# Row maxima of a 256 MB matrix: one load queue in place of two, and a last tile that ends in both of its rows

## The chip, the cores and the metric

The kernel runs on one core of a Trainium2 chip. The metric is the device time of that core in microseconds (us). Before the change three runs gave 630.47, 630.69 and 630.90, a median of 630.69. One further execution is recorded by the hardware profiler, and the profile below is that one.

## The reference

The input `x` is a float32 matrix of 8192 rows and 8192 columns, 268 MB. The output is one float32 for each row: the largest absolute value in it.

```python
def reference(x):
    return np.linalg.norm(x, ord=np.inf, axis=1)
```

Every element is read from memory once and takes part in one comparison. 32 KB are written.

## The kernel before

**Tiling.** The 8192 rows are spread over the 128 partitions of the on-chip memory (SBUF), 64 rows to a partition. A tile `t` holds two rows of each partition (`B` = 2), 16384 columns of 4 bytes, so 8.39 MB. There are 32 tiles. Three buffers of the pool `sbuf` take turns (`BUFS` = 3), and each has 16 spare columns at its end (`PAD`). A buffer is loaded again when the reduce of its last use has ended.

**Bulk.** The first 24 tiles (six groups of four, `A` = 6 and `G` = 4) are loaded by one transfer each at L146. VectorE (DVE in the profile) then reduces each with one instruction at L139, `reduce_max` with absolute values, to two results per partition in `r_bulk`. L145 chooses the queue of the load. Tiles 1 to 11 are issued by ScalarE, which has no other work, and tile 0 and tiles 12 to 23 by SyncE (SP). The 48 results per partition are stored at L151, from ScalarE.

**Tail.** The last eight tiles are loaded in pieces, on SP, at L159. The list `TAIL` gives the widths of the pieces: a tile's 16384 columns are the two rows one after the other, and `segments` cuts a piece at the border between the rows. Each segment gets a reduce of its own. For the first fifteen rows of the tail the partial maxima go to `part`, one column for each segment; a reduce of 15 x 4 values makes `r_tail` of it, and ScalarE stores it at L171. The last row's partial maxima are written into the spare columns behind the row itself, so that the final reduce, `r_fin`, takes the last load and the six partial maxima in one instruction. SP stores it at L179.

**What orders the work.** Each engine works through its instructions in the order of the program. SP does nothing but issue transfers. A load waits on SP for its buffer to come free. A transfer announces its landing on one of eight semaphores, handed out in turn, and so it also waits for the transfer that had the same semaphore eight transfers earlier. The stores count among these.

**Start and end.** `start_first_load_early` moves SP's first load ahead of the barrier at the program's start. `finish_on_pool` lets the GpSimd engine wait for the last store. Both stay as they are.

Of the kernel before, what the change touches and what calls it, by code (L numbers as in the profile page):

```python
# [1 line left out]
logging.getLogger("concourse").setLevel(logging.ERROR)  # L3

# [1 line left out]

# [4 lines left out]

F32 = mybir.dt.float32
X = mybir.AxisListType.X

TAIL = [
    [2944, 13440],
    [4096, 12288],
    [11520, 4864],  # L20
    [7680, 8704],
    [6528, 3328, 6528],
    [4864, 4096, 3328, 4096],
    [3968, 3584, 3328, 2944, 2560],
    [2432, 2176, 1920, 1664, 1536, 1280, 1152, 1024, 1152, 1024, 1024],
]


def segments(loads, cols):

    out, at = [], 0
    for i, w in enumerate(loads):
        end = at + w
        while at < end:
            r = at // cols
            to = min(end, (r + 1) * cols)
            out.append((i, r, at - r * cols, to - at))
            at = to
    return out


def start_first_load_early(nc):


    sp = mybir.EngineType.SP
    first, *rest = nc.main_func.blocks
    for block in rest:
        insts = block.instructions
        for i, ins in enumerate(insts):
            if ins.engine == sp and type(ins).__name__ == "InstDMACopy":  # L50
                assert not ins.sync_info.on_wait
                moved = insts[i]
                block.instructions = insts[:i] + insts[i + 1 :]
                head = first.instructions
                at = next(k for k, h in enumerate(head) if h.engine == sp)
                first.instructions = head[:at] + [moved] + head[at:]
                return


def finish_on_pool(nc):  # L60

    sp, pool = mybir.EngineType.SP, mybir.EngineType.Pool
    body, end = nc.main_func.blocks[-2:]
    last_store = [
        i
        for i in body.instructions
        if i.engine == sp and type(i).__name__ == "InstDMACopy"
    ][-1]  # L70
    lane = last_store.sync_info.on_update[0].id
    insts = end.instructions
    src = next(i for i in insts if i.engine == sp)
    assert type(src).__name__ == "InstDrain" and not src.sync_info.on_update
    at = next(k for k, i in enumerate(insts) if type(i).__name__ == "InstISA")
    drain, clear = insts[at - 1], insts[at]
    assert drain.engine == clear.engine == pool
    assert type(drain).__name__ == "InstDrain"
    assert not (drain.sync_info and drain.sync_info.on_wait)
    waits = sorted(src.sync_info.on_wait, key=lambda s: s.id == lane)  # L80
    assert waits[-1].id == lane
    wait = mybir.InstDrain(
        name=nc.get_next_instruction_name(),
        engine=pool,
        ins=[],
        outs=[],
        sync_info=mybir.SyncInfo(on_wait=waits, on_update=[]),
    )
    moved = {src.name, drain.name, clear.name}
    end.instructions = [i for i in insts if i.name not in moved] + [wait, clear]  # L90


@with_exitstack
def kernel(
    ctx: ExitStack,
    tc: tile.TileContext,
    x: bass.AP,
    out: bass.AP,
    G: int = 4,
    B: int = 2,  # L100
    BUFS: int = 3,
    PAD: int = 16,
):
    nc = tc.nc
    P = nc.NUM_PARTITIONS
    rows, cols = x.shape
    W = B * cols


    n_tail = B * len(TAIL)  # L110
    n_bulk_rows = rows // P - n_tail
    assert n_bulk_rows % (G * B) == 0
    A = n_bulk_rows // (G * B)
    split = n_bulk_rows * P
    x_b = x[:split].rearrange("(a p n b) c -> a n p (b c)", p=P, a=A, n=G, b=B)
    out_b = out[:split].rearrange("(a p n b) -> p a (n b)", p=P, a=A, n=G, b=B)
    x_t = x[split:].rearrange("(p t b) c -> t p (b c)", p=P, b=B)
    out_t = out[split:].rearrange("(p t) -> p t", p=P)

    sbuf = ctx.enter_context(tc.tile_pool(name="sbuf", bufs=BUFS))  # L120
    outp = ctx.enter_context(tc.tile_pool(name="outp", bufs=1))

    segs = [segments(loads, cols) for loads in TAIL]
    count = {}
    for i, s in enumerate(segs):
        for _, r, _, _ in s:
            count[i * B + r] = count.get(i * B + r, 0) + 1
    n_last = count[n_tail - 1]
    k_max = max(count[r] for r in range(n_tail - 1))
    assert n_last - 1 <= PAD  # L130

    r_bulk = outp.tile([P, A, G * B], F32)
    r_tail = outp.tile([P, n_tail], F32)
    r_fin = outp.tile([P, 1], F32)
    part = outp.tile([P, n_tail - 1, k_max], F32)
    nc.vector.memset(part[:], 0.0)  # L136

    def absmax(o, i):
        nc.vector.reduce_max(out=o, in_=i, axis=X, apply_absolute_value=True)  # L139

    for a in range(A):
        for n in range(G):
            t = sbuf.tile([P, W + PAD], F32, tag="t")
            i = a * G + n
            queue = nc.scalar if 1 <= i < A * G // 2 else nc.sync  # L145
            queue.dma_start(out=t[:, :W], in_=x_b[a, n])  # L146
            absmax(
                r_bulk[:, a, n * B : (n + 1) * B],
                t[:, :W].rearrange("p (b c) -> p b c", b=B),
            )  # L150
    nc.scalar.dma_start(out=out_b, in_=r_bulk[:])  # L151

    seen = {}
    for i, loads in enumerate(TAIL):
        t = sbuf.tile([P, W + PAD], F32, tag="t")
        todo = segs[i]
        at = 0
        for j, w in enumerate(loads):
            nc.sync.dma_start(out=t[:, at : at + w], in_=x_t[i][:, at : at + w])  # L159
            at += w  # L160
            for _, b, c, n in [s for s in todo if s[0] == j]:
                r = i * B + b
                k = seen.get(r, 0)
                seen[r] = k + 1
                lo = b * cols + c
                if r < n_tail - 1:
                    absmax(part[:, r, k : k + 1], t[:, lo : lo + n])
                    if r == n_tail - 2 and k == count[r] - 1:

                        absmax(r_tail[:, : n_tail - 1], part[:])  # L170
                        nc.scalar.dma_start(  # L171
                            out=out_t[:, : n_tail - 1], in_=r_tail[:, : n_tail - 1]
                        )
                elif k < n_last - 1:
                    absmax(t[:, W + k : W + k + 1], t[:, lo : lo + n])
                else:

                    absmax(r_fin[:], t[:, lo : W + n_last - 1])
    nc.sync.dma_start(out=out_t[:, n_tail - 1 :], in_=r_fin[:])  # L179
    nc.at_finalize(start_first_load_early)  # L180
    nc.at_finalize(finish_on_pool)


# [1 line left out]
_INS = ['x']  # L185
_OUTS = [((8192,), 'float32')]


# [23 lines left out]
```

## Time and profile before

| | before |
|---|---|
| median of three runs | 630.69 us |
| profiled execution, device time | 630.47 us |
| profiled execution, span from first to last instruction | 628.3 us |
| VectorE busy | 551.5 us, 88% of the span |
| 24 bulk reduces (L139, 128x16384) | 411.9 us, 17214 ns each |
| 31 reduces into `part` | 130.2 us |
| 6 reduces into the last tile, and `r_fin` | 7.9 us and 1.2 us |
| VectorE idle before bulk reduces, waiting for loads | 73.4 us |
| mean rate of the transfers | 427 GB/s |
| share of SP's queue and of ScalarE's | 65.3% and 34.1% of 16 engines' span |

The page gives busy time and idle time for each engine, and rows of 40 slices in which a digit is the busy share in tenths. A group of instructions is shown with the line of the code, the engine, what is written from what, the shape, and what ended the idle time before it. A transfer has a time of issue and a time from issue to landing, which includes its turn in the queue. The names SPq and ACTq stand for the instruction queues of SP and ScalarE. The profiled execution's device time is 2.2 us longer than its span.

### The profile page before, as it was taken

The numbers are of one execution on the slowest core, as the hardware profiler recorded it, in microseconds if no ns is written. First come the engines' busy times: TensorE is split into PE (matmuls) and PEld (weight loads), VectorE is DVE, ScalarE is ACT, GpSimd is POOL, SyncE is SP. The second block draws the span as 40 slices with busy tenths as digits, with TensorE's granted clock in tenths as the row PEclk, the third lists the DMA queues.
The fourth block names the chain that finished last, engine by engine and source line by source line (L and its number), as shares of the span: only waits on it lengthen the run. The fifth ranks groups of instructions, "written<-read, shape, count | busy, mean of one in ns | idle before, by whom it ended". The sixth has DMA issues, their size and how long they took to land.

```text
span 628.3 us, 202 instructions
## 1 busy us (share of the span) xinstructions
DVE 551.5 (88%) x64; POOL 0.2 (0%) x4
## 2 busy tenths in 40 slices
DVE  0059999999998880799999999988889999999998
POOL 0000000000000000000000000000000000000000
DMA  9999999999999999999999999999999999999997
GB/s 401 467 401 467 401 451 417 413 455 413 455 421 446 421 446 426 442 401 455 413 451 417 446 421 446 421 446 421 434 432 410 439 440 423 424 433 429 424 423 299
DMA packets 8993, 268.48 MB, mean 427 GB/s; under 512 B 1952, under 2 KB 1952, under 8 KB 3104
## 3 DMA queue, kind: packets, MB, share of 16 engines
q1 hardware_dynamic: 6480, 176.16, 65.3%
q10 hardware_dynamic: 2512, 92.31, 34.1%
q14 instruction: 1, 0.01, 0.0%
HBM read 268.44 MB, written 0.03 MB: 427 GB/s over the span
## 4 chain that ended last, share of the span: by engine, by line
DVE 62%; DMA 32%; another core or an unknown queue 3%; issue 2%; SPq 0%
DVE r_bulk L139 47%; DMA t<-in_x_dram 32%; DVE part L139 14%; DVE t L139 1%; DVE r_fin L139 0%; SPq L159 0%; DVE r_tail L139 0%
## 5 line engine op out<-in xcount | busy, mean ns | idle before, releaser
L139 DVE TENSOR_REDUCE r_bulk<-t 128x2 f32<-128x16384 f32 x24 | 411.9, 17214 | 73.4 <-DMA t<-in_x_dram 73.4
L139 DVE TENSOR_REDUCE part<-t 128x1 f32<-128x8192 f32 (+18 forms) x31 | 130.2, 4272 | 0.7 <-DMA t<-in_x_dram 0.6
L139 DVE TENSOR_REDUCE t<-t 128x1 f32<-128x1152 f32 (+3 forms) x6 | 7.9, 1387 | 0.0
L139 DVE TENSOR_REDUCE r_fin<-t 128x1 f32<-128x1030 f32 x1 | 1.2, 1226 | 0.0
L136 DVE MEMSET part<- 128x60 f32 x1 | 0.1, 108 | 0.9 <-PEq L196 0.9
L139 DVE TENSOR_REDUCE r_tail<-part 128x15 f32<-128x60 f32 x1 | 0.2, 216 | 0.0
L196 POOL MEMSET const-bfloat16-1.0<- 128x1 bf16 x1 | 0.1, 101 | 0.0
L196 POOL MEMSET const-uint8-127<- 128x1 uint8 x1 | 0.1, 101 | 0.0
L196 POOL MEMSET const-float32-0.0<- 128x1 f32 x1 | 0.1, 98 | 0.2 <-issue 0.2
L196 POOL MEMSET const-float32-1.0<- 128x1 f32 x1 | 0.1, 98 | 0.0
## 6 DMA issues: line engine op xcount, KB each, us to landing
t<-in_x_dram SPq DMA_DIRECT2D x1, 6720.0 KB, 40.4
t<-in_x_dram SPq DMA_DIRECT2D x2, 3264.0 KB, 26.3
t<-in_x_dram SPq DMA_DIRECT2D x3, 2048.0 KB, 28.7
t<-in_x_dram SPq DMA_DIRECT2D x1, 6144.0 KB, 40.6
t<-in_x_dram SPq DMA_DIRECT2D x1, 5760.0 KB, 35.2
t<-in_x_dram SPq DMA_DIRECT2D x3, 1664.0 KB, 32.3
t<-in_x_dram SPq DMA_DIRECT2D x2, 2432.0 KB, 32.4
t<-in_x_dram SPq DMA_DIRECT2D x1, 4352.0 KB, 43.0
```

Of the source, the lines that this page charges most:

```text
L136: nc.vector.memset(part[:], 0.0)
L139: nc.vector.reduce_max(out=o, in_=i, axis=X, apply_absolute_value=True)
L196: nc = _bacc.Bacc("TRN2", target_bir_lowering=False, num_devices=1)
```

## The change

All 24 bulk loads are issued by SP (L145 in the new file), so ScalarE issues only the store of the bulk results.

The tail's first seven tiles have new piece widths. The last tile leaves the list `TAIL` and gets the list `LAST` of 13 loads, each of one row alone: four of row 0, seven of row 1, and then one last load of 640 columns for each row. These two are placed at the end of the buffer, row 0's first, each followed in SBUF by that row's partial maxima (four and seven). The final reduces of the two rows take the last load and the partial maxima together, and write straight into `r_tail`.

The reduce of `part` to `r_tail` (14 x 4 values now) stands behind the first piece of the last tile. One store on SP takes all 16 tail results of each partition; the store of fifteen rows on ScalarE and `r_fin` go.

```diff
 TAIL = [
-    [2944, 13440],
-    [4096, 12288],
-    [11520, 4864],
-    [7680, 8704],
-    [6528, 3328, 6528],
-    [4864, 4096, 3328, 4096],
-    [3968, 3584, 3328, 2944, 2560],
-    [2432, 2176, 1920, 1664, 1536, 1280, 1152, 1024, 1152, 1024, 1024],
+    [9728, 6656],
+    [5632, 10752],
+    [9600, 6784],
+    [9344, 7040],
+    [6784, 6528, 3072],
+    [4736, 3072, 4224, 4352],
+    [3968, 2432, 3072, 2944, 1792, 2176],
 ]
+LAST = (
+    [(0, w) for w in (2176, 2048, 1664, 1664)]
+    + [(1, w) for w in (1536, 1280, 1152, 1024, 896, 896, 768)]
+    + [(0, 640), (1, 640)]
+)
...
-            i = a * G + n
-            queue = nc.scalar if 1 <= i < A * G // 2 else nc.sync
-            queue.dma_start(out=t[:, :W], in_=x_b[a, n])
+            nc.sync.dma_start(out=t[:, :W], in_=x_b[a, n])
...
+    t = sbuf.tile([P, W + PAD], F32, tag="t")
+    left = parts_of[:]
+    col = [0] * B
+    at, slot = 0, {}
+    ends = [w for _, w in LAST[-B:]]
+    lo = W - sum(ends)
+    for b in range(B):
+        slot[b] = lo + ends[b]
+        lo = slot[b] + parts_of[b]
+    for j, (b, w) in enumerate(LAST):
+        final = left[b] == 0
+        to = slot[b] - w if final else at
+        frm = b * cols + col[b]
+        nc.sync.dma_start(out=t[:, to : to + w], in_=x_t[len(TAIL)][:, frm : frm + w])
+        col[b] += w
+        if final:
+            r = n_tail - B + b
+            absmax(r_tail[:, r : r + 1], t[:, to : slot[b] + parts_of[b]])
+        else:
+            left[b] -= 1
+            k = slot[b] + left[b]
+            absmax(t[:, k : k + 1], t[:, to : to + w])
+            at += w
+        if j == 0:
+            absmax(r_tail[:, : n_tail - B], part[:])
+    nc.sync.dma_start(out=out_t, in_=r_tail[:])
-    nc.sync.dma_start(out=out_t[:, n_tail - 1 :], in_=r_fin[:])
```

## The prediction

> **What bounds the kernel now.** I read the page from the top: busy shares and slices first, then the waits of the vector engine, then the order of time around the one long wait, then the queue's own waits, then the end.
>
> ```profile
> span 628.3 us, 202 instructions
> DVE 551.5 (88%) x64; POOL 0.2 (0%) x4
> DVE  0059999999998880799999999988889999999998
> DMA  9999999999999999999999999999999999999997
> HBM read 268.44 MB, written 0.03 MB: 427 GB/s over the span
> ```
>
> The DMA row is full in every slice but the last, while the vector engine (DVE) starts two slices late and has thin places. So the input stream sets the time: what counts is when the last load lands, and what follows it. DVE idle time costs nothing unless it delays a load. In order of time, DVE alone, the steady state and the odd place:
>
> ```profile
> 196.70 17.22 DVE L139 TENSOR_REDUCE r_bulk<-t 128x2 f32<-128x16384 f32 x1 [2.13 <-DMA t<-in_x_dram]
> 215.98 17.22 DVE L139 TENSOR_REDUCE r_bulk<-t 128x2 f32<-128x16384 f32 x1 [2.06 <-DMA t<-in_x_dram]
> 254.69 85.72 DVE L139 TENSOR_REDUCE r_bulk<-t 128x2 f32<-128x16384 f32 x5 [21.49 <-DMA t<-in_x_dram]
> ...
> 449.75 17.22 DVE L139 TENSOR_REDUCE r_bulk<-t 128x2 f32<-128x16384 f32 x1 [2.08 <-DMA t<-in_x_dram]
> 469.15 17.22 DVE L139 TENSOR_REDUCE r_bulk<-t 128x2 f32<-128x16384 f32 x1 [2.18 <-DMA t<-in_x_dram]
> ```
>
> Where DVE waits for each tile, tiles come 19.3 to 19.4 us apart ((469.15-411.10)/3 = 19.35 us, the start at 411.10 being the same view's). DVE needs 17.2. All 32 tiles at 19.35 would take 619.2 us. The last load, issued at 615.19, took 9.9 and landed at 625.1; so 5.9 us were lost somewhere. At 215.98 the queues change hands: the last load of ScalarE's queue (issued 194.60, 60.1 us to landing) and the first of SP's (issued 213.94, 40.9) share the engines and land together at 254.7 and 254.8. DVE is starved for 21.49 us, so it frees the next buffer late, and SP issues its third load of this series only at 271.94, with the load before it (issued 233.23, 40.7) landing at 274.0. The windows show what that does:
>
> ```profile
> 256.00:272.00 16.00, 16.00 (x2) 0.00 (x0) 1.00 1.04 451
> 272.00:278.00 6.00, 6.00 (x1) 0.00 (x0) 1.00 0.90 350
> 278.00:294.00 16.00, 16.00 (x2) 0.00 (x0) 1.00 1.05 455
> ```
>
> The last two columns are DMA share and GB/s: for 6 us the stream runs at 0.90 and 350. (Short windows read some 20 GB/s to either side of the 433 that 8.39 MB in 19.35 us make.) By landings the hole is 271.94+22.84 = 294.78 against 273.96, that is 20.82 us for one tile: 1.45 more than 19.37. No later tile gives it back. The other losses: start, 2.5 (two loads landed by 41.2 against 38.7); the fifth and sixth tile, 0.6 (80.02 to 119.32 against 38.7); the eight tail tiles, 1.2 (469.13 to 625.14 against 154.8). With 1.45 that is 5.75 of the 5.9.
>
> SP's own waits, and the end:
>
> ```profile
> SPq L159 <- DMA t<-in_x_dram: 62.6, 19, 7.4
> SPq L159 <- DMA out_dram<-r_bulk: 25.5, 1, 25.5
> ```
>
> SP stood 25.5 us behind the bulk store (486.40, 60.5 us to landing). This is a wait for the semaphore that the store had used, eight transfers earlier in the program. One load of 6528 columns was still queued (issued 521.01, 33.5 to landing: 554.5) when the store landed at 546.9, so the stream did not dry up.
>
> ```profile
> 621.71 3.59 DVE L139 TENSOR_REDUCE t<-t 128x1 f32<-128x1024 f32 x3
> 625.34 1.23 DVE L139 TENSOR_REDUCE r_fin<-t 128x1 f32<-128x1030 f32 x1
> 626.59 0.34 SPq L179 DMA_DIRECT2D out_dram<-r_fin  x1
> ```
>
> The last reduce starts 0.20 us after the last landing (625.14), held by the reduce before it (ends 625.30); it ends at 626.57; the store issues at 626.59, lands 1.41 later at 628.00, and the span ends at 628.27.
>
> **What the Trainium skill says.** "DMA: Bandwidth & Descriptors", Issuing engines are not separate DMA queues: transfers from several engines run on the same 16 DMA engines and interleave. The trace agrees: the twelfth and thirteenth load land 0.17 us apart, and neither queue alone is slower than both (19.32 us a tile on ScalarE's, 19.35 on SP's). Same page, Queues, rings and completion order: each engine takes turns between queues. That fits the 60.5 us of a 24 KB store behind six loads. "VectorE: DVE Perf Modes", The perf-mode tier table: `tensor_reduce` has only the 1x program, so the cost follows the element count; here (8678-1208)/(8192-1024) = 1.042 ns an element and 0.141 us fixed, of which about 0.08 overlaps the neighbour (six reduces of 8.32 in sum were busy 7.91).
>
> **The change, part by part.**
>
> *All 24 bulk loads on SP.* Removed: eleven issues on ScalarE (0.33 us each, hidden). Added: eleven on SP, in order, each behind its buffer wait. SP has nothing else to do, so what queues behind them is only the next load. Tile k+3 is issued when DVE ends tile k, 17.24 us after k landed; two tiles, less 17.2 us of progress, are still queued: 38.7-17.2 = 21.5 us of work. This is the state of 409 to 469 in the trace (issue to landing 40.7), with no hole. There is no handover any more, so two loads never land together, and the hole of 1.45 goes. At the start loads land singly: the first near 22 us instead of 38.8. DVE then starts early and idles 2.1 us a tile; hidden by the stream, worth nothing. Bounds: 0 if a hole comes elsewhere, -1.45 for this one, -2.1 if the 0.6 of the fifth and sixth tile goes too (seen only while ScalarE's queue ran, cause unknown). I take **-1.45**.
>
> *New tail pieces.* The tail has 34 loads instead of 31. Eleven loads in the last tile cost 19.67 against 19.35: 0.03 a load; **+0.1**. I followed the new widths through, at 1.195 ns a column for the stream and the reduce prices above, with three buffers and the wait for the transfer eight before. The second load of the fifth tail tile (6528) now stands behind the bulk store. The store again has six loads beside it (5632 to 7040), and a load of 6784 columns (8.1 us) is in the queue when it lands; before it was 6528 (7.7 us). The cover is as good. DVE last waits for a landing at the start of the seventh tail tile and then keeps a backlog of 0.1 to 0.5 us, two small reduces of slack.
>
> *The last two loads.* Reduces of 768 and 640 columns take 0.86 and 0.73 us start to start, against landings 0.77 apart, so the last reduce starts about 0.35 after the last landing (0.20 before). It has 640+7 elements: 0.141+0.674 = 0.815 us, instead of 1.23. From last landing to end of reduce: 1.17 instead of 1.43, **-0.26**. Both final reduces also wait for DVE's own earlier writes; those are at least one reduce back, so I count nothing; if they break the overlap it is +0.16.
>
> *One store.* ScalarE's store of fifteen rows goes (it took 5.3 us beside the loads, off the path; the 0.22 us reduce before it moves ahead in the tile). The final store has 64 bytes a partition instead of 4. No row shows such a store on idle engines; between 0 and +0.2, set against up to 0.1 regained from the store that no longer cuts into the last loads. I take **0**.
>
> Sum: -1.45+0.10-0.26 = -1.61. The profiled execution took 630.47 (span 628.27 and 2.2 around it), so 628.9; the median shown is 0.22 higher, so about **629.0**. A difference under 0.2% (1.26 us) can't be told from none.
>
> **Rivals.**
>
> (a) *The hole is not regained*: a single queue gets a hole of the same size elsewhere, at a tail issue say, or the last engine lags anyway. Then only the end improves, -0.16: 630.5. For it: the trace has unexplained slow places (the 0.6). Against: none in the stretch 294 to 469, where SP works alone.
>
> (b) *The slow place goes as well*: another -0.6 to -0.7, 628.3. For: it is only in ScalarE's stretch. Against: ScalarE's stretch from 119 to 216 runs at 19.32.
>
> (c) *Slower: SP is stuck behind the bulk store until the stream is dry.* Place: the wait of the 6528-column load. If the store lands as the 6784-column load does, the next load meets empty engines. Price: an issue 2.0 us before the running load landed cost 1.45, so an issue at its landing costs about 3.5; -1.61+3.5 gives 632.6. It decides against the change from a store about 7.5 us later than the end of the 7040-column load. For: packets of the six loads differ in size, so the turns fall differently. Against: the total beside the store is the same (six loads), and it would have to lose nearly a whole further load.
>
> (d) *The change does not do what it says*: the new final reduces wait for each other and the end gains nothing; with the hole closed that is 629.2, inside the forecast.
>
> **How the numbers follow.** Forecast with (d) 0.58, (b) 0.14, (a) 0.18, (c) 0.08, other mishaps 0.02. The likeliest case has 628.4 to 629.7; (b) reaches 628.0, (a) 630.6; the range 628.0 to 630.6 leaves out (c) and little else. Faster means under 629.43: most of the forecast and all of (b), 0.68. Within 0.2%: the forecast's upper edge and (a), 0.22. Slower: (c) and mishaps, 0.10.
>
> **What would show it.** Right: every bulk tile waits 2.1 us for its load, starts 19.35 apart from the first (near 22 us) to the twenty-fourth (near 467.5); no idle of 21 us, no window at 350 GB/s in mid-stream; last landing near 623.8; last reduce about 0.82 us, its end 1.2 after that landing; span near 626.7. Wrong: a bulk start over 20 us after its neighbour, a DMA share under 0.95 before the end (near 547 for (c)), DVE waiting in the last tile, or a final store well over 1.41 us.

## The result, and the profile after

| | before | after |
|---|---|---|
| median of six runs, us | 630.94 (630.47 to 632.19) | 627.98 (627.73 to 628.23) |
| profiled execution, device time, us | 630.47 | 628.23 |
| its span, us | 628.3 | 626.4 |

The change makes the kernel faster: the ratio is 0.9949, with a 95% interval of 0.9936 to 0.9962, which is 3.0 us in the medians. The forecast was 629.0, from 628.0 to 630.6. The direction was right; the gain was under-estimated by about 1 us, and the measured time lies just under the lower end. Already visible in the table: the times before are spread over 1.7 us, those after over 0.5.

The page after, the same lines as shown of before (a row of digits is the busy share in tenths, in 40 slices):

```profile
span 626.4 us, 204 instructions
DVE 552.9 (88%) x67; POOL 0.2 (0%) x4
DVE  0588988889988889888898888988889999999998
DMA  9999999999999999999999999999999999999997
HBM read 268.44 MB, written 0.03 MB: 429 GB/s over the span
```

The transfers are still what fills the time, and DVE is as busy as before (552.9 us against 551.5). It starts one slice earlier and is idle evenly, not in lumps. The order of time of DVE shows it:

```profile
215.62 17.22 DVE L140 TENSOR_REDUCE r_bulk<-t 128x2 f32<-128x16384 f32 x1 [2.08 <-DMA t<-in_x_dram]
234.99 17.22 DVE L140 TENSOR_REDUCE r_bulk<-t 128x2 f32<-128x16384 f32 x1 [2.15 <-DMA t<-in_x_dram]
254.34 17.22 DVE L140 TENSOR_REDUCE r_bulk<-t 128x2 f32<-128x16384 f32 x1 [2.12 <-DMA t<-in_x_dram]
273.64 17.22 DVE L140 TENSOR_REDUCE r_bulk<-t 128x2 f32<-128x16384 f32 x1 [2.08 <-DMA t<-in_x_dram]
293.00 17.22 DVE L140 TENSOR_REDUCE r_bulk<-t 128x2 f32<-128x16384 f32 x1 [2.14 <-DMA t<-in_x_dram]
...
466.99 17.22 DVE L140 TENSOR_REDUCE r_bulk<-t 128x2 f32<-128x16384 f32 x1 [2.14 <-DMA t<-in_x_dram]
```

Each tile waits some 2.1 us for its load. The wait of 21.49 us is gone, and the last bulk tile starts at 466.99, where it started at 469.15 before. The three windows of which the middle one read 350 GB/s before (last two columns: DMA share, GB/s):

```profile
256.00:272.00 16.00, 15.55 (x1) 0.00 (x0) 1.00 0.95 414
272.00:278.00 6.00, 4.36 (x1) 0.00 (x0) 1.00 1.13 492
278.00:294.00 16.00, 13.86 (x2) 0.00 (x0) 1.00 0.94 406
```

These windows do not measure a hole, neither here nor in the prediction. The stream is made of packets of 64 KB, which take 2.42 us each on one of 16 engines, and a window counts a packet in full where it starts. A window of 6 us therefore holds two packets of each engine, 350 GB/s, or up to three, 524. Over all 38 us the kernel before reads 437 GB/s with its hole, and the changed one 423 without. What shows the hole is the landings: 273.96 and 294.78 before, 20.8 us apart, and 273.61 and 292.98 now, 19.4 apart (DVE starts 0.02 to 0.03 us after each of these two). Among SP's waits, the one for the bulk store is nearly as long as before:

```profile
SPq L158 <- DMA out_dram<-r_bulk: 24.3, 1, 24.3
```

The store landed at 543.3 (issued 484.24, 59.1 us), while a load that landed at 552.7 was still in the queue. The end, in order of time:

```profile
617.90 5.31 DVE L140 TENSOR_REDUCE t<-t 128x1 f32<-128x1152 f32 x5
623.13 1.55 DVE L140 TENSOR_REDUCE r_tail<-t 128x1 f32<-128x644 f32 x2
624.71 0.35 SPq L192 DMA_DIRECT2D out_dram<-r_tail  x1
```

The last load was issued at 614.70 and landed after 8.9 us, at 623.61. The two final reduces run from 623.13 to 624.68 without a gap, and the store of all 16 results lands 1.4 us after its issue.

### The profile page after: what moved, and what is told of

Same layout as the page of the kernel before. It is cut to its first block, busy times and chain, and to the rows that moved or that the text cites. A ratio compares the mean times of both kernels' runs of the same rounds, so it can differ in the third digit from the quotient of the medians.

```text
span 626.4 us, 204 instructions
## 1 busy us (share of the span) xinstructions
DVE 552.9 (88%) x67; POOL 0.2 (0%) x4
## 4 chain that ended last, share of the span: by engine, by line
DMA 63%; DVE 35%; issue 1%; another core or an unknown queue 0%; DVEq 0%
DMA t<-in_x_dram 63%; DVE r_bulk L140 24%; DVE part L140 8%; DVE t L140 3%; DVEq L220 0%; DVE r_tail L140 0%
## 5 line engine op out<-in xcount | busy, mean ns | idle before, releaser
L140 DVE TENSOR_REDUCE part<-t 128x1 f32<-128x8192 f32 (+20 forms) x28 | 121.6, 4410 | 0.9 <-DMA t<-in_x_dram 0.8
L140 DVE TENSOR_REDUCE t<-t 128x1 f32<-128x1664 f32 (+8 forms) x11 | 16.5, 1572 | 0.0
L140 DVE TENSOR_REDUCE r_tail<-t 128x1 f32<-128x644 f32 (+1 forms) x2 | 1.5, 814 | 0.0
```

## Experiments

The theory at this point (A in the expectations, L once it is narrowed to the late issue): the two queues of the kernel before cause the loss, in one place. When ScalarE's last load and SP's first overlap they land together; DVE is starved, the next buffer comes free late, and a load is issued when the stream is nearly dry. Below, the *lead* of a load is the time from its issue to the landing of the load before it, and its *hole* is what its landing comes late: its time from issue to landing, less the lead, less the 19.35 us of a tile. The rivals: the time is saved in the tail (B), or the hole belongs to the change of queue itself and not to the late issue (Q). Times of the kernel before that stand in a comparison were measured beside the run they are compared with.

### The two halves of the change

One queue, all else as before:

```diff
-            queue = nc.scalar if 1 <= i < A * G // 2 else nc.sync
+            queue = nc.sync
```

> The kernel before with one edit: all bulk loads on SP; tail and stores as before. Theory A (the two queues cost the time: a hole of 1.45 us at the handover and 0.6 in the fifth and sixth tile): span about 626.3, no DVE wait over 3 us after the first tile, tiles 19.35 apart throughout, 2.0 to 2.5 us less than the kernel before. Theory B (the time is saved in the tail and at the end, the queues do not matter): same time as before, within 0.3 us, with another hole somewhere in the stream.

Measured: 628.28 us (628.02 to 628.64) against 631.13 for the kernel before, ratio 0.9958 (0.9945 to 0.9972): 2.85 us less. The span of the profiled execution is 626.7, the longest wait after the first tile 2.3 us. B falls: the choice of queue alone has nearly the whole gain, and somewhat more than I expected. Some 0.3 us of it lies outside the span, as the last experiment takes up.

The other half, the new tail with the old queues:

```diff
-            nc.sync.dma_start(out=t[:, :W], in_=x_b[a, n])
+            i = a * G + n
+            queue = nc.scalar if 1 <= i < A * G // 2 else nc.sync
+            queue.dma_start(out=t[:, :W], in_=x_b[a, n])
```

> The changed kernel with the old choice of queues: tiles 1 to 11 on ScalarE, the new tail, the last tile with two final reduces and one store. Theory A: the 21 us wait at the thirteenth tile and the window at 350 GB/s two tiles later are back; 0.2 to 0.5 us less than the kernel before, all of it at the end. Theory B: 2 us or more less than before.

Measured: 630.22 us against 631.13, ratio 0.9990 (0.9982 to 0.9998). The hole is back, 1.8 us in this profile. The 0.9 us is more than expected; the interval allows 0.1 to 1.1. About 0.3 of it lies outside the span here too: the device time is 1.8 us longer than the span in all 13 runs of this kernel, mostly 2.0 to 2.2 in those of the kernel before.

The kernel before once more, for a second profile:

> The kernel before, unchanged, for a second profile on the chip of the other runs and for the spread of its time. Theory A: the hole two tiles after the handover is there again, 1.4 us or more, and if its time is 1 us longer than in the first profile, the hole or the slow place after the start is what grew. Theory B: the time varies in other places.

Measured: 630.87 us, ratio 0.9999 (0.9991 to 1.0007). The hole is again at the load issued at 271.9, but bigger (columns: queue, number, us to landing):

```profile
t<-in_x_dram SPq DMA_DIRECT2D x1, 23.7
```

In the first profile it took 22.8, so the hole is 2.35 instead of 1.45. The slow place in the fifth and sixth tile, 0.6 before, is under 0.1 here. So the same code has holes of different size, and the slow place is not in every execution.

### Is it the late issue?

Two handovers from a full queue:

```diff
-            queue = nc.scalar if 1 <= i < A * G // 2 else nc.sync
+            queue = nc.scalar if 4 <= i < 15 else nc.sync
```

> The kernel before with the queue of the bulk loads changed twice from a full queue: tiles 0 to 3 on SP, 4 to 14 on ScalarE, 15 to 23 on SP. Theory A (a change of queue lets two loads land together, starves DVE for 21 us, and the next buffer comes free only 2 us before the stream is dry): two waits of 21 us, two holes of about 1.4 us each, none of the slow start; 2.9 us slower than the run with one queue, about 0.6 to 0.9 slower than the kernel before. Theory B: the same time as before. If the hole was an accident of one place, one hole at most.

Measured: 629.67 us, 1.5 us less than before (ratio 0.9981, 0.9971 to 0.9991), and 1.4 more than with one queue, of which 0.3 lies outside the span. Both waits are there, 20.91 and 21.48 us. But the first handover, from SP to ScalarE, left a lead of 2.6 us and no hole; the second left 2.0 us and a hole of 0.6. My expectation was wrong: two handovers are not two holes.

Next, all as before, but the buffer freed 2.1 us earlier by leaving columns out of one reduce:

```diff
+            cut = 1024 if i == 11 else 0
             absmax(
                 r_bulk[:, a, n * B : (n + 1) * B],
-                t[:, :W].rearrange("p (b c) -> p b c", b=B),
+                t[:, :W].rearrange("p (b c) -> p b c", b=B)[:, :, : cols - cut],
             )
```

> The kernel before, queues as before; only the reduce of the twelfth tile (the last on ScalarE's queue) leaves out the last 1024 columns of both rows, 2048 of 16384, so that DVE frees its buffer 2.1 us earlier and the next load is issued about 4.1 us instead of 2.0 us before the stream would be dry. Theory L (the hole is the late issue): the two loads still land together and DVE still waits 21 us, but the hole is gone; 2.0 to 2.6 us less than the kernel before. Theory Q (the hole belongs to the change of queue itself): the hole stays, the time within 0.3 us of before.

Measured: 628.59 us against 631.11, ratio 0.9958 (0.9946 to 0.9971), 2.5 us less. In its order of time on DVE the starved wait is unchanged:

```profile
215.44 17.22 DVE L139 TENSOR_REDUCE r_bulk<-t 128x2 f32<-128x16384 f32 x1 [2.07 <-DMA t<-in_x_dram]
254.15 83.59 DVE L139 TENSOR_REDUCE r_bulk<-t 128x2 f32<-128x14336 f32 x5 [21.48 <-DMA t<-in_x_dram]
```

and the load issued when the shortened reduce ended, at 269.3, has no hole:

```profile
t<-in_x_dram SPq DMA_DIRECT2D x1, 23.5
```

Its 23.5 us are the lead of 4.2 and the 19.35 of a tile. The queues, the handover and the 21 us of idle DVE are those of before. Only the issue came 2.1 us earlier, and the hole went. So it is the late issue (L), not the change of queue, and a 21 us wait of DVE by itself costs nothing here.

The opposite, the buffer freed 2.2 us later:

```diff
+            if i == 11:
+                absmax(part[:, 0, 0:1], t[:, :2048])
```

> The kernel before, queues as before; DVE reduces 2048 columns of the twelfth tile a second time (2.2 us, into a place that is written again later), so that the next load is issued when the stream is just running dry. Theory L: the hole grows by about the same 2.2 us, to about 4.5; 2 us slower than before. Theory Q: the hole keeps its size, since DVE has idle time enough; time within 0.3 us of before.

Measured: 631.49 us against 631.11, ratio 1.0004 (0.9996 to 1.0012), the same within its interval. The lead is -0.2 us, and the load took

```profile
t<-in_x_dram SPq DMA_DIRECT2D x1, 22.0
```

from issue to landing, just as the first load of a kernel with one queue does (21.9 to 22.1); the hole is 2.8. I had expected a hole of 4.5 and 2 us more. Leads of 2.0 showed up to 2.35 in the profiles so far, and the medians differ by 0.4: the loss does not follow the lateness one for one. Taken alone, this run is nearer to what Q forecast (within 0.3); what speaks against Q is the shortened reduce above and the run with one queue below.

Two points between:

```diff
-            cut = 1024 if i == 11 else 0
+            cut = 256 if i == 11 else 0
```

> The kernel before; the reduce of the twelfth tile leaves out the last 256 columns of both rows, so that the next load is issued 2.5 us before the stream would be dry. Theory L with a limit between 2.0 and 2.6 us (an issue 2.6 us ahead lost nothing in the run with two handovers): no hole or one under 0.3 us, 2 us or more less than before. If the loss falls evenly from 2.0 to 4.2 us: a hole of 1.0 to 1.8 us is left.

Measured: 630.90 us against 631.04, ratio 0.9994 (0.9987 to 1.0002). With a lead of 2.5 the load took

```profile
t<-in_x_dram SPq DMA_DIRECT2D x1, 24.7
```

so the hole is 2.8, as big as in the run where the stream did run dry. The sharp limit between 2.0 and 2.6 that I expected is not there.

```diff
-            cut = 1024 if i == 11 else 0
+            cut = 576 if i == 11 else 0
```

> The kernel before; the reduce of the twelfth tile leaves out the last 576 columns of both rows, so that the next load is issued about 3.2 us before the stream would be dry. If the limit is at the time from issue to a new load's first packets, [...]no hole and 628.6; if the loss falls slowly up to 4.2 us, a hole of 0.5 to 2 us.

Measured: 629.19 us against 630.90, ratio 0.9969 (0.9958 to 0.9979). A lead of 3.2 and a hole of 0.4 in the profile; the median lies 0.6 above that of the lead of 4.2. Part of the loss is left, nearer to the second alternative, whose lower end was 0.5.

These four kernels and the kernel before differ in one reduce alone, so their medians, of 5 to 14 executions each where a profile is one, can be set side by side. Against the kernel before, whose lead is 2.0, they gain 2.5 us at a lead of 4.2, 1.7 at 3.2 and 0.1 at 2.5, and lose 0.4 at -0.2. Most of the loss appears between 3.2 and 2.5.

### Is a second queue needed for a hole?

One queue, with one buffer held back by extra reduces (here with the second, 2048-column one):

```diff
             queue = nc.sync
...
+            if i == 5:
+                absmax(part[:, 0, 0:1], t[:, :W])
+                absmax(part[:, 1, 0:1], t[:, :2048])
```

> One queue throughout; DVE reduces the whole sixth tile and 2048 columns of it once more (19.4 us, into places that are written again later), so that one load, that of the ninth tile, is issued about 2.0 us before the stream would be dry, with no other queue in use. Theory L (a nearly dry stream costs the time, whoever made it so): a hole of 1.4 to 2.8 us at the ninth tile, and as much slower than the run with one queue, near 630.5. Theory Q (the mixing of two queues is needed): no hole beyond the 0.6 us that a load from an empty queue would show.

Measured: 630.45 us, ratio to before 0.9990 (0.9981 to 0.9999), and 2.2 us slower than one queue without the delay. In its order of time on DVE, the extra reduces and what follows:

```profile
118.71 17.22 DVE L139 TENSOR_REDUCE r_bulk<-t 128x2 f32<-128x16384 f32 x1 [2.11 <-DMA t<-in_x_dram]
135.84 19.40 DVE L139 TENSOR_REDUCE part<-t 128x1 f32<-128x16384 f32 x2
155.16 85.71 DVE L139 TENSOR_REDUCE r_bulk<-t 128x2 f32<-128x16384 f32 x5
```

and the one load issued then, at 155.3 (columns: queue, number, us to landing):

```profile
t<-in_x_dram SPq DMA_DIRECT2D x1, 23.0
```

With a lead of 2.1 that is a hole of 1.5 us, of the size seen at the handovers, with no other queue in use. The spread of its times is 1.8 us, like that of the kernel before. Its control, with the large reduce alone:

> Control of the run with one queue and a late buffer: only the second reduce of the whole sixth tile (17.2 us), so that the load is issued about 4.2 us ahead. No hole in either theory; the time of the run with one queue, 628.3.

Measured: 628.14 us, ratio 0.9956 (0.9942 to 0.9971): a lead of 4.3, no hole, and the time of the run with one queue. DVE had 17.2 us of extra work at no cost in time. A second queue is not needed for a hole; in the kernel before, the handover was what made the buffer late.

### The place of the handover

```diff
-            queue = nc.scalar if 1 <= i < A * G // 2 else nc.sync
+            queue = nc.scalar if 1 <= i < 20 else nc.sync
```

> The kernel before with the queues changing hands at tile 20 instead of tile 12. Theory L: the wait of 21 us and the hole move with it, to tiles 19 and 22; the same time as before within 0.4 us. Theory P (the hole belongs to a place in the matrix or in time): it stays near 273 us or is gone.

Measured: 637.50 us, 6.4 slower than before (ratio 1.0099, 1.0085 to 1.0112). The hole moved as expected, to the load issued at 426.7 (22.8 us, lead 2.0, 1.4 us). What I had not expected is in the order of time on DVE:

```profile
409.45 85.72 DVE L139 TENSOR_REDUCE r_bulk<-t 128x2 f32<-128x16384 f32 x5 [21.76 <-DMA t<-in_x_dram]
495.09 129.92 DVE L139 TENSOR_REDUCE part<-t 128x1 f32<-128x2944 f32 x31
625.05 0.22 DVE L139 TENSOR_REDUCE r_tail<-part 128x15 f32<-128x60 f32 x1
```

After the wait of 21.76 us DVE never waits again. It is the bound to the end: 224.9 us of work from 409.45 to 634.35, while the last load landed at 627.1. A wait of 21 us is free only while enough of the stream remains to make it up, at 2.1 us a tile.

```diff
-            queue = nc.scalar if 1 <= i < A * G // 2 else nc.sync
+            queue = nc.scalar if 1 <= i < 10 else nc.sync
```

> The kernel before with the queues changing hands at tile 10 instead of tile 12, while the queue has not yet filled again after the start (a load is issued some 15 us before the one ahead of it lands, not 21). Theory L: the two loads overlap only in part, the following load is issued some 6 us before the stream would be dry, and there is no hole; 2.0 to 2.6 us less than before, close to the run with one queue. Theory Q: a hole as before and the time of before.

Measured: 628.04 us (628.01 to 628.06) against 631.11, ratio 0.9948 (0.9934 to 0.9961). With the queue only partly filled at the handover the lead is 4.5 (I had expected some 6), and there is no hole. The kernel before is 3 us faster by the number 10 in place of 12, with both queues kept; 0.3 of that lies outside the span.

The same with the new tail:

> The changed kernel with the queues of the run that handed over at tile 10: two queues, no hole, and the new tail. If only the hole made two queues slower, it is as fast as the changed kernel, 627.7 to 628.0; if a second queue costs something of its own beside the hole, it is 0.5 us or more slower.

Measured: 628.30 us against 631.04, ratio 0.9956 (0.9943 to 0.9968), and beside it the changed kernel itself:

> The changed kernel again, for its time and its spread on the chip of these runs: 628.0 with a spread under 0.6 us, 3 us less than before. Its span ends 1.8 us before the device time does, against 2.2 in most runs of the kernel before.

Measured: 627.91 us (627.74 to 628.60), ratio 0.9950 (0.9937 to 0.9962). Between the two alternatives for the second queue's own cost, 0.4 us apart in the medians with overlapping ranges, this does not decide. With the old tail the sign is the opposite: the handover at 10 has 628.04, one queue 628.28. So no cost of a second queue beyond the hole is seen. No version tried is faster than the changed kernel by more than the runs can tell.

### What lies outside the span

The device time is longer than the span by 2.2 us in most runs of the kernel before and by 1.8 in all runs of the changed one. The runs with one queue, with the new tail and with the handover at 10 or 20 have 1.8 too, the shorter and the longer reduce mostly 2.2. SP's instruction stream differs in length between these kernels, so I lengthened it (the two more cuts also give DVE two more reduces):

```diff
-    [2944, 13440],
-    [4096, 12288],
+    [2944, 6720, 6720],
+    [4096, 6144, 6144],
```

> The kernel before with two more loads on SP: the 13440 columns of the first tail tile in two loads of 6720, the 12288 of the second in two of 6144. The stream, the hole and the end should not change (0.1 us for two loads). If the 0.3 us by which device time and span stand further apart in the kernel before depend on where SP's instruction stream ends, the distance is 1.8 here in all runs and the time 0.3 us less than before; if it belongs to the last store or the stream of loads, it stays at 2.2.

Measured: the distance is 1.79 to 1.89 in all 14 runs, as the first alternative said. But the time is 630.99 us against 631.04, ratio 1.0000 (0.9990 to 1.0009), with a hole of 2.6 in the profile: a gain of 0.3 in the whole is neither seen nor excluded.

## Why the prediction was right and where it was wrong

**What bounds the kernel** was right: the stream, and one place in it. The hole was rightly read from the landings; the windows at 350 GB/s, taken as a second sign of it, show only how many packets started in 6 us. The last landing moved by 1.5 us (625.14 to 623.61; predicted 623.8), and the span by 1.9 (predicted 1.6).

**The hole of 1.45** had the right cause, a buffer that comes free late after the handover, but the wrong size, and this is the step that failed: the term -1.45 of the sum. I took it from one execution. That execution, at 630.47, was one of the quicker: the medians of the kernel before beside the experiments are 630.9 to 631.1. Six other profiles of a handover with a lead of 2.0 to 2.5 us show 2.35, 1.8, 0.6, 1.4, 2.8 and 2.6; with the first, their mean is 1.9. The run that removes the hole and nothing else (lead 4.2) gains 2.5, and its times are spread over 0.8 us. So the term was about -2.5 and not -1.45 (why the medians give more than the mean of the profiles is not shown): an effect that varies between executions is not measured by one profile. My bounds for it, 0 to -2.1, did not contain it either; the lower end came from adding another loss of the same profile, not from asking how large the hole can be.

**The 2.2 us around the span** I carried over unchanged. After the change they are 1.8. That is 0.35 us of the difference between the profiled executions, and the prediction put it at nothing.

**The slow fifth and sixth tile** (rival b) does not belong to ScalarE's queue: it is missing in the second profile of the kernel before, and one of the same size, 0.55 us over two tiles, stands early in the profile of the control above, where SP alone issues.

**The tail's +0.1** was 0.6 between the two profiles: from the last bulk landing to the last landing of all the changed kernel took 156.6 us (466.97 to 623.61), before 156.0. But the old tail takes 156.3 in the profile with one queue and up to 156.6 in others, so the new widths alone are not shown to cost 0.6. 0.5 of it was one load: it landed at 584.15, 5.7 us after the one before it, where its 4352 columns make 5.2. The profiles of the two other runs with the new tail and no hole have the same 5.7, the one with the hole has 5.2.

**The end's -0.26** was -0.36: the last reduce started 0.25 after its load and ended 1.07 after it. The two final reduces overlapped their neighbours, so rival (d) did not come about. The store cost 1.43 instead of 1.41; taking 0 was right. What the new tail is worth as a whole is not settled, in medians of kernels that were not run side by side: with one queue in both it gains 0.3 to 0.4 us (628.28 to 627.98 and 627.91), with the handover at 10 in both it loses 0.3 (628.04 to 628.30).

In medians: 2.5 for the hole and 0.35 outside the span make 2.85, which is what one queue alone gained; measured for the whole change were 3.0 and, in the last comparison, 3.1. The 0.15 to 0.25 that is left for tail and end is within what the runs can tell. The part outside the span is argued from the distances, since the run made for it did not show it in the time.

**Rivals.** (a), the hole comes back elsewhere, is refuted by the run with one queue. (c), SP stuck behind the bulk store until the stream is dry: the wait was 24.3 us, but the store landed 9.4 us before the load that covered it. Its price was wrong too: an issue as the stream runs dry was put at 3.5 us, and the longer reduce showed 2.8 in the profile and 2.9 against the lead of 4.2 in the medians. Rival (a) had the second largest chance, and it pulled the range up; nothing stood for a larger hole.

## What to carry to other kernels

Where a stream of loads bounds a kernel, look at the smallest lead: how long before the queue runs dry the next load is issued. In these profiles 4 us lost nothing, and 2 us lost 0.6 to 2.6 us each time it occurred; in these runs a handover, a long reduce and a held buffer all cost time through that lead. A consumer's idle time is free only until the work behind it no longer fits beside the remaining stream. And a loss seen in one profile is a sample: compare the spread of the runs before and after, and profile twice, before taking its size for a forecast.

## What was not expected of the hardware

| lead, us | kernel | issue to landing, us | hole, us |
|---|---|---|---|
| -0.2 | longer reduce | 22.0 | 2.8 |
| 2.0 | before, first and second profile | 22.8, 23.7 | 1.45, 2.35 |
| 2.0 | two queues with the new tail; longer SP stream | 23.2, 24.0 | 1.8, 2.6 |
| 2.0 | handover at 20 | 22.8 | 1.4 |
| 2.0 | second of two handovers | 22.0 | 0.6 |
| 2.1 | one queue, late buffer | 23.0 | 1.5 |
| 2.5 | shortened by 256 columns | 24.7 | 2.8 |
| 2.6 | first of two handovers, to ScalarE's queue | 22.0 | 0 |
| 3.2 | shortened by 576 columns | 23.0 | 0.4 |
| 4.2 | shortened by 1024 columns | 23.5 | 0 |
| 4.3 | one queue, control | 23.6 | 0 |
| 4.5 | handover at 10 | 23.9 | 0 |

A load of 8.39 MB into an empty queue lands after 22.0 us. One that is issued 2.0 to 2.5 us before the stream runs dry takes 22 to 24.7, and can lose as much as if the stream had stopped.

The records of the single packets show part of what happens. They fall into 16 chains, in which each packet starts as the one before it ends; I take each chain for one engine. In the full stream a packet of 64 KB takes 2.42 us. Around a load with a lead of 2.0 to 2.5, chains stand still for a while, and the packets after that take up to 3.2 to 3.8 us. The 16 chains lose 0.6 to 1.6 us on average, but the slowest of them loses 1.3 to 3.5. A load has landed only when all 16 are done, and the hole goes with the slowest: 2.2 us for the hole of 1.45, 3.5 for that of 2.35, 1.3 for that of 0.6. With leads of 3.2 to 4.5, and at the handover with 2.6, no chain loses more than 0.5. In the first load of the changed kernel, into an empty queue, the first packets start 1.0 to 1.6 us after the issue and take about 3.0.

Why one chain comes so much later than the others, why this varies between executions, and whether ScalarE's queue differs (one profile at 2.6 without a loss) stay open.

The distance between device time and span changes by 0.35 us between kernels that differ in what SP issues: the run made for it has 1.8, and so have the runs with one queue and with the handover at 10 or 20, whose DVE work is that of the kernel before. It does not simply follow the number of SP's transfers: 37 (handover at 20) and 47 (at 10) give 1.8, 45 (before) gives 2.2. The packet records hold a clue. In every profile with 2.2, and in the second one of the kernel before with 2.1, a transfer of 8 KB of instructions starts 1.9 us after the end of the span; in those with 1.8 the last one starts at most 0.5 us after it, or before it. The two handovers, with 2.1 and no such late transfer, do not fit, and no run was made to test it.
